# Building the S5 input matrices of six units on GpSimd instead of VectorE, in halves, with their transposes later on TensorE

## The chip, the cores and the metric

One core of a Trainium2 chip runs one program. Its engines are TensorE (PE in the profile: matrix products and transposes, with PEld for weight loads), VectorE (DVE), ScalarE (ACT), GpSimd (POOL) and SyncE (SP, which here only issues DMAs). Each engine takes its own instructions in order and waits on semaphores for the others. The metric is device time in microseconds for the whole program. Before the change: 1237.72 us, the median of three runs (1236.06 to 1237.88).

## The reference, cut to what matters

The program is a two-layer decoder trunk on 512 tokens of width 1024: an S5 state-space mixer, a gated FFN, stick-breaking attention and a second FFN. The change lies in the S5 mixer alone. It has 64 groups of 16 channels, each with 64 complex diagonal states:

```python
u = (h @ w_in).reshape(bsz, seq, N_GROUPS, SSM_GROUP)
mag = jnp.exp(a_re * dt)
ab_re, ab_im = mag * jnp.cos(a_im * dt), mag * jnp.sin(a_im * dt)
...
bb_re = f_re[..., None] * b_re - f_im[..., None] * b_im
bb_im = f_re[..., None] * b_im + f_im[..., None] * b_re
bu_re = jnp.einsum('blgh,gph->blgp', u, bb_re)
bu_im = jnp.einsum('blgh,gph->blgp', u, bb_im)
...
_, _, s_re, s_im = lax.associative_scan(combine, (a_seq_re, a_seq_im, bu_re, bu_im), axis=1)
y = (jnp.einsum('blgp,ghp->blgh', s_re, c_re) - jnp.einsum('blgp,ghp->blgh', s_im, c_im)
     + d_skip * u)
y = jax.nn.gelu(y.reshape(bsz, seq, D_SSM))
z = y @ w_glu
return z[..., :D_MODEL] * jax.nn.sigmoid(z[..., D_MODEL:])
```

## The kernel before

The scan is not run token by token. The 512 tokens are cut into 64 chunks of 8. Within a chunk everything is a matrix product with matrices made from the powers of the state factors: `b` with powers 1 to 8 gives the matrix that turns 8 inputs into a chunk's contribution to the state, `c` with powers 0 to 7 the one that turns a state into 8 outputs, and both together a small Toeplitz matrix for the part inside the chunk. Only the states from chunk to chunk are scanned.

The work is split into eight units n = 0 to 7 of eight groups each. For one unit:

- `op_b(n)` makes the input matrices. `products` multiplies `b3` (real, imaginary and a combination) by `pw3` (powers, 1 to 8) into a tile k of 1536 elements a partition; `sums` adds pairs of its thirds into bn, 1024 elements (a complex product with three real ones). Both on VectorE.
- `bt_(n, 0)` and `bt_(n, 1)` transpose the real and the imaginary half of bn on TensorE into PSUM bank kb; ScalarE copies each to a tile bts. `v_(n)` then multiplies bts with the inputs u8.
- `op_c(n)` makes cm in the same way from `c3`; `kk(n)` makes the Toeplitz kernel from cm (also in bank kb), ScalarE copies it into kx, `kx_(n)` adds the skip term on VectorE and sends it through DRAM (ks) into the matrix m by DMAs on SP.
- `states(n)` on VectorE: p (v turned by the table tb), wv, the scan rv with the decay tile mt, p again, then xv, the states at the chunk starts.
- `y_in(n)` (u8 with m) and `y_state(n)` (xv with cm) fill the output bank y on TensorE; ScalarE applies the gelu; `y_turn` transposes back, ScalarE splits the result into yh and yl, with a product yt<-yh,nid between them in `y_low`.

TensorE's own filler work is the product u = h @ w_in (`u` in the profile) and later the first part of the gated output product (`gl`). `fill(k)` puts k steps of it at a place; the table F says how many at four places of each unit, after the states (F[n][0]), after `y_state`, after `y_turn` and after `y_low`.

In the loop over n, the order on TensorE, VectorE and ScalarE is exactly the order in which the code is written (a manual schedule). GpSimd and SP are not in it: their order is set by the framework's scheduler. Unit n of the loop runs kk and v of unit n + 1, states and outputs of unit n, and op_b, bt_ and op_c of unit n + 2; before the change the five steps of `states(n)` and the two of `op_b(n + 2)` take turns. Units 0 and 1 are prepared ahead of the loop. bn has one buffer, so bn of a unit can be written only when the transposes of the unit before have read it. GpSimd, before the change, only writes zeros (the first part of kx, the first column of each block of mt and xv, once a unit) and issues the loads of w_in (wi) and w_glu (wvr).

Of the kernel before, what the change touches and what calls it, by code (L numbers as in the profile page):

```python
# [7 lines left out]
F32 = mybir.dt.float32  # L8
# [5 lines left out]
MUL, ADD, SUB, MAX, MIN = ALU.mult, ALU.add, ALU.subtract, ALU.max, ALU.min  # L14
# [3 lines left out]
P = 128  # L18
# [24 lines left out]
def bc(ap, axis, shape):  # L43
    return ap.unsqueeze(axis).to_broadcast(shape)
# [3 lines left out]
def trunk(ctx: ExitStack, tc: tile.TileContext, A, out):  # L48
    nc = tc.nc
    V, SC, PE, GP = nc.vector, nc.scalar, nc.tensor, nc.gpsimd  # L50
# [32 lines left out]
    def T(name, dt=F32, tag=None):  # L83
        if tag in TP:
            return tp.tile([P, S], dt, tag=tag, name=name, bufs=TP[tag])
        pool, bufs = cur["w"]
        return pool.tile([P, S], dt, tag=tag, name=name, bufs=bufs[tag])
# [4 lines left out]
    def wide(name, n, tag):  # L92
        pool, bufs = cur["w"]
        return pool.tile([P, n * S], F32, tag=tag, name=name, bufs=bufs[tag])
# [16 lines left out]
    def tt(o, a, b, op, eng=None):  # L111
        (eng or V).tensor_tensor(out=o, in0=a, in1=b, op=op)  # L112
# [128 lines left out]
    def s5(st_next):  # L241
        banks_by_tag(st=1, u=2, g=2, kb=1, v=1, y=1)
        with tc.tile_pool(name="s5", bufs=1) as sp, ExitStack() as wctx:
            def L(name, shape, bufs=None, dt=F32):
                return sp.tile([P] + shape, dt, name=name, **({"bufs": bufs} if bufs else {}))
# [6 lines left out]
            def halves(t):  # L252
                return t[:, 0:S], t[:, S:2 * S]
# [4 lines left out]
            b3, c3 = L("b3", [32, 3, 16]), L("c3", [32, 3, 16])  # L258

            def v4(t, a=4):  # L260
                return t.rearrange("p (a b) -> p a b", a=a)
# [90 lines left out]
            def fill(n):  # L352
                for _ in range(n):
                    next(pe)
# [43 lines left out]
            zc, k, r, p = s32(), s32(), s32(), s32()  # L398
# [73 lines left out]
            pw3 = L("pw3", [32, 3, 9])  # L472
# [39 lines left out]
            mg8 = L("mg8", [32])  # L512
# [13 lines left out]
            V.memset(tb[:, 1, :, 0:1], 0.0)  # L526
            sp2 = wctx.enter_context(tc.tile_pool(name="s5w", bufs=2))

            sh8 = [P, 4, 8, 16]

            def v5(t):
# [34 lines left out]
            def products(m3, pw3, n, e0):  # L566

                pr = slice(4 * n, 4 * n + 4)
                k3 = wide("k", 3, "k")
                sh = [P, 12, 8, 16]  # L570
                tt(k3.rearrange("p (a e h) -> p a e h", a=12, e=8), bc(m3[:, pr].rearrange("p a t h -> p (a t) h"), 2, sh),
                   bc(pw3[:, pr].rearrange("p a t e -> p (a t) e")[:, :, e0:e0 + 8], 3, sh), MUL)
                return k3.rearrange("p (a t c) -> p a t c", a=4, t=3)

            def sums(o, k3):

                o4 = o.rearrange("p (r a c) -> p r a c", r=2, a=4)
                tt(o4, bc(k3[:, :, 0], 1, [P, 2, 4, P]), k3[:, :, 1:3].rearrange("p a t c -> p t a c"), ADD)
# [8 lines left out]
            def kk(n):  # L587

                cmr, cmn = unit[n]["c"]
                bk = B("kk", "kb")  # L590
                for q in range(4):
                    o = bk[32 * q:32 * q + 32, 0:128]
                    mm(o, bdr[:, 4 * n + q], v4(cmr)[:, q], True, False)
                    mm(o, bdi[:, 4 * n + q], v4(cmn)[:, q], False, True)
                kx = sp2.tile([P, 240], F32, name="kx", bufs=1)
                GP.memset(kx[:, 0:112], 0.0)
                SC.copy(out=kx[:, 112:240], in_=bk[:, 0:128])
                unit[n]["kx"] = kx

# [14 lines left out]
            def op_b(n):  # L614

                unit[n] = {}
                k3 = products(b3, pw3, n, 1)
                yield
                bn = wide("bn", 2, "bn")
                sums(bn, k3)  # L620
                unit[n]["b"] = halves(bn)

            def bt_(n, i):
                pb = B("bt", "kb")
                for q in range(4):
                    PE.transpose(v4(pb)[:, q], v4(unit[n]["b"][i])[:, q], ident)
                bt = T("bts", tag="bt")
                SC.copy(out=bt, in_=pb)
                unit[n].setdefault("bt", []).append(bt)
# [10 lines left out]
                               v4(bts[ri])[:, q, 64 * g2:64 * g2 + 64], u83[:, 2 * q + g2], True, True)  # L640
                unit[n]["v"] = vb

            decay = {}

            def decays(n):

                decay[n] = sp2.tile([P, 256], F32, name="mt", bufs=1)
                m4 = v4(decay[n])
                SC.copy(out=m4, in_=bc(mg8[:, 4 * n:4 * n + 4], 2, [P, 4, 64]))
                GP.memset(m4[:, :, 0:1].rearrange("p q o -> p (q o)"), 0.0)  # L650

            def states(n):

                pr = slice(4 * n, 4 * n + 4)
                vb = unit[n].pop("v")
                turn = tb[:, :, pr].rearrange("p t q c -> p t (q c)")
                sh2 = [P, 2, 2, 256]
                p = wide("p", 2, "p")
                p4 = p.rearrange("p (t r c) -> p t r c", t=2, r=2)
                a1, a2 = p4[:, 0], p4[:, 1]  # L660
                tt(p4, bc(v4(vb, 2), 1, sh2), bc(turn, 2, sh2), MUL)
                yield
                wv = T("wv", tag="wv")
                tt(wv[:, 0:256], a1[:, 0], a2[:, 1], ADD)
                tt(wv[:, 256:512], a1[:, 1], a2[:, 0], SUB)
                yield
                rv = T("rv", tag="rv")
                for ri in range(2):
                    c = slice(256 * ri, 256 * ri + 256)
                    V.tensor_tensor_scan(out=rv[:, c], data0=decay[n], data1=wv[:, c], initial=0.0, op0=MUL, op1=ADD)  # L670
                if n + 1 < KT:
                    decays(n + 1)
                yield
                p = wide("p", 2, "p")
                p1, p2 = halves(p)
                tt(p.rearrange("p (t r c) -> p t r c", t=2, r=2), bc(v4(rv, 2), 1, sh2), bc(turn, 2, sh2), MUL)
                yield
                xv = T("xv", tag="xv")
                xv4 = xv.rearrange("p (r q c) -> p r q c", r=2, q=4)
                GP.memset(xv4[:, :, :, 0:1].rearrange("p r q o -> p (r q) o"), 0.0)  # L680
                r1 = p1.rearrange("p (r q c) -> p r q c", r=2, q=4)
                r2_ = p2.rearrange("p (r q c) -> p r q c", r=2, q=4)
                tt(xv4[:, 0, :, 1:64], r1[:, 0, :, 0:63], r2_[:, 1, :, 0:63], SUB)
                stt(xv4[:, 1, :, 1:64], r1[:, 1, :, 0:63], -1.0, r2_[:, 0, :, 0:63], MUL, SUB)

                unit[n]["x"] = xv4
# [36 lines left out]
            def y_low(yt, yh, yl):  # L723
                mm(yt, nid, yh, False, False)
                SC.copy(out=yl, in_=yt)
                ys.append((yh, yl))

            def run(gen, n=99):
                for _ in range(n):
                    if next(gen, True) is True:  # L730
                        return

            run(op_b(0))
            op_c(0)
            kk(0)
            evac()
# [5 lines left out]
            run(table, TAB0)  # L742
            evac()
            v_(0)
            run(op_b(1))
            fill(PRE[3])
            bt_(1, 0)
            bt_(1, 1)
# [5 lines left out]
            fill(PRE[4])  # L754
            evac()
            decays(0)
            with tc.manual_schedule(engines={E.PE, E.DVE, E.Activation}):
                for n in range(KT):
                    more = n + 2 < KT
                    if n + 1 < KT:  # L760
                        kk(n + 1)
                        v_(n + 1)
                    if n and n + 1 < KT:
                        turn_products(n + 1)
                    y_in(n)
                    st, cb = states(n), op_b(n + 2) if more else iter(())
                    for i in range(5):
                        run(st, 1)
                        run(cb, 1)
                        if i == 2:  # L770
                            if n + 1 < KT:
                                kx_(n + 1)
                            prep_lo()
                        if i == TSUM and n + 1 < KT:
                            turn_sums(n + 1)
                    fill(F[n][0])
                    y8 = y_state(n)
                    if more:
                        bt_(n + 2, 0)
                    evac(n == 0)  # L780
                    if more:
                        op_c(n + 2)
                    fill(F[n][1])
                    yy = y_turn(y8)
                    if more:
                        bt_(n + 2, 1)
                    fill(F[n][2])
                    y_low(*yy)
                    fill(F[n][3])
                    if n:  # L790
                        prep_hi(1)
# [699 lines left out]
```

## Time and profile before

| | before |
|---|---|
| median of three runs | 1237.72 us |
| profiled execution: device time | 1236.96 us |
| its span in the trace | 1235.2 us |
| granted TensorE clock | 0.997 |
| the loop over the units | about 58 to 155 us of the span |

In the profile, an instruction is named by line, engine, operation and its tiles, output and inputs (`bn<-k`). Line 112 is the helper `tt` (two-input VectorE instruction), 109 `stt`, 106 `mm`; so tiles tell more than lines. A busy time is the time in which an engine has an instruction under way; an entry in square brackets at the end of a row is the idle time before the instruction and what ended it. Starts of consecutive instructions overlap a little, so the cost of an instruction in a full queue is the distance from its start to the next start. In the tables by stretch, the columns are the stretch, its length, and for PE, PEld, DVE, ACT and POOL the busy time with the number of instructions, then the granted clock, the DMA share and GB/s.

### The profile page before, as it was taken

The numbers are of one execution on the slowest core, as the hardware profiler recorded it, in microseconds if no ns is written. First come the engines' busy times: TensorE is split into PE (matmuls) and PEld (weight loads), VectorE is DVE, ScalarE is ACT, GpSimd is POOL, SyncE is SP. The second block draws the span as 40 slices with busy tenths as digits, with TensorE's granted clock in tenths as the row PEclk, the third lists the DMA queues.
The fourth block names the chain that finished last, engine by engine and source line by source line (L and its number), as shares of the span: only waits on it lengthen the run. The fifth ranks groups of instructions, "written<-read, shape, count | busy, mean of one in ns | idle before, by whom it ended". The sixth has DMA issues, their size and how long they took to land.

```text
span 1235.2 us, 16227 instructions
## 1 busy us (share of the span) xinstructions
PE 1207.6 (98%) x6411; PEld 982.8 (80%) x6411; DVE 809.6 (66%) x1284; ACT 539.3 (44%) x866; POOL 24.2 (2%) x65
## 2 busy tenths in 40 slices
PE   7989999999999999999999999999999999999995
PEld 3457788788888888888889898888888888888884
DVE  7999764665435635557878989878655346536554
ACT  5234453433223323334577878765433233323331
POOL 1011020000000000000000000000000000000000
PEclk9999999999999999999999999999999999999998
DMA  5565443233233233233211211123233232332322
GB/s 199 150 166 140 122 124 98 86 102 98 90 102 99 82 106 101 92 91 100 76 51 53 82 55 48 39 86 103 86 102 97 91 103 86 91 113 88 94 75 69
DMA packets 55068, 118.47 MB, mean 96 GB/s; under 512 B 12912, under 2 KB 28528, under 8 KB 54992
## 3 DMA queue, kind: packets, MB, share of 16 engines
q1 hardware_dynamic: 50880, 105.55, 27.9%
q0 software_dynamic: 3248, 11.54, 3.1%
q8 instruction: 50, 0.82, 0.3%
q10 hardware_dynamic: 864, 0.35, 0.1%
q14 instruction: 26, 0.21, 0.1%
HBM read 109.03 MB, written 8.39 MB: 95 GB/s over the span
## 4 chain that ended last, share of the span: by engine, by line
PE 89%; DVE 8%; ACT 1%; issue 1%; DMA 1%; SPq 0%; DVEq 0%; ACTq 0%
PE fd L106 20%; PE fu L106 19%; PE fg L106 19%; PE kqb L106 7%; PE gl L106 6%; PE z L106 5%; PE ob L106 5%; PE v L106 4%; DVE k L112 2%; DVE p L112 1%; PE u L106 1%; PE y L106 1%; DVE cm L112 1%; DVE u L112 1%; DVE rv L670 1%
## 5 line engine op out<-in xcount | busy, mean ns | idle before, releaser
L106 PE MATMUL fd<-ah,wdh 128*128 128x512 f32 (+1 forms) x359 | 140.5, 391 | 0.0
L106 PE MATMUL fd<-ah,wdl 128*128 128x512 f32 (+1 forms) x359 | 139.2, 388 | 0.0
L106 PE MATMUL fd<-al,wdh 128*128 128x512 f32 (+1 forms) x359 | 137.9, 384 | 0.0
L112 DVE TENSOR_TENSOR x<-x,fd 128x512 f32<-128x512 f32 (+1 forms) x49 | 33.1, 676 | 119.8 <-PE fd L106 119.8
L157 ACT CAST wuh<-wur 128x1024 fp32r<-128x1024 f32 x44 | 46.4, 1054 | 134.4 <-PE fg L106 118.0
L157 ACT CAST wdh<-wdr 128x896 fp32r<-128x896 f32 (+1 forms) x48 | 47.1, 982 | 128.0 <-PE fd L106 98.2
L112 DVE TENSOR_TENSOR g<-fg,rb 128x512 f32<-128x512 f32 x44 | 30.4, 691 | 96.3 <-PE fg L106 93.5
L106 PE MATMUL fu<-xh,wuh 128*128 128x512 f32 x220 | 86.0, 391 | 0.0
L106 PE MATMUL fg<-xh,wgl 128*128 128x512 f32 x220 | 85.8, 390 | 0.0
L106 PE MATMUL fg<-xh,wgh 128*128 128x512 f32 x220 | 85.7, 390 | 0.0
L106 PE MATMUL fg<-xl,wgh 128*128 128x512 f32 x220 | 85.6, 389 | 0.0
L106 PE MATMUL fu<-xh,wul 128*128 128x512 f32 x220 | 85.6, 389 | 0.0
L106 PE MATMUL fu<-xl,wuh 128*128 128x512 f32 x220 | 85.6, 389 | 0.0
L112 DVE TENSOR_TENSOR u<-fu,rb 128x512 f32<-128x512 f32 x44 | 30.4, 691 | 80.5 <-PE fu L106 80.5
L106 PE MATMUL fu<-xhl,wuh 128*128 128x512 f32 x264 | 81.8, 391 | 0.0
L106 PE MATMUL fg<-xhl,wgh 128*128 128x512 f32 x264 | 81.5, 389 | 0.0
L106 PEld LDWEIGHTS fd<-ah,wdl 128*128 128x128 f32 x359 | 67.4, 188 | 15.2
L106 PEld LDWEIGHTS fd<-al,wdh 128*128 128x128 f32 x359 | 67.4, 188 | 14.8 <-issue 0.2
L106 PEld LDWEIGHTS fd<-ah,wdh 128*128 128x128 f32 x359 | 67.5, 188 | 13.2 <-issue 0.2
L157 ACT CAST wgh<-wgr 128x1024 fp32r<-128x1024 f32 x44 | 46.3, 1053 | 71.0 <-PE fd L106 33.0
L106 PE MATMUL u<-xg,wi 128*128 128x512 f32 x128 | 63.5, 628 | 7.5 <-ACT xg L270 7.5
L109 DVE SCALAR_TENSOR_TENSOR acc<-g,cw,acc 128x511 f32<-128x511 f32 x88 | 65.8, 747 | 2.4 <-ACT acc L832 0.9
(247 smaller groups left out, 2799.1 us busy)
## 6 DMA issues: line engine op xcount, KB each, us to landing
wgr<-in_w_up SPq DMA_DIRECT2D x44, 512.0 KB, 3.5
wur<-in_w_up SPq DMA_DIRECT2D x44, 512.0 KB, 3.5
wdr<-in_w_dn SPq DMA_DIRECT2D x32, 448.0 KB, 3.3
wdr<-in_w_dn SPq DMA_DIRECT2D x16, 512.0 KB, 3.5
wvr<-in_w_glu POOLq DMA_DIRECT2D x12, 512.0 KB, 3.8
ks<-kx SPq DMA_DIRECT2D x32, 128.0 KB, 2.5
m<-ks SPq DMA_DIRECT2D x8, 512.0 KB, 4.1
awr<-in_w_k SPq DMA_DIRECT2D x8, 512.0 KB, 3.5
```

The lines of the kernel that those rows point to most:

```text
L106: PE.matmul(o, lhsT=lhsT, rhs=rhs, start=start, stop=stop, skip_group_check=True)
L109: (eng or V).scalar_tensor_tensor(out=o, in0=a, scalar=s, in1=b, op0=op0, op1=op1)
L112: (eng or V).tensor_tensor(out=o, in0=a, in1=b, op=op)
L157: SC.copy(out=hi, in_=raw)
L670: V.tensor_tensor_scan(out=rv[:, c], data0=decay[n], data1=wv[:, c], initial=0.0, op0=MUL, op1=ADD)
```

## The change

For n = 2 to 7, `op_b` makes bn on GpSimd in two halves (two of the unit's four state blocks each): a product kp of 768 elements into a buffer of its own, and a sum of 512 elements into half of bn. For n = 0 and 1 VectorE still does it. kx, mt and xv become tiles that exist once: their zeros are written once ahead of the loop, and the per-unit zero fills on GpSimd are gone; the ScalarE copy into mt leaves the zero column out (63 of 64 columns). In the loop, `op_b(n + 2)` stands ahead of `states(n)`; `bt_(n + 2, 0)` moves from behind `y_state` to behind `y_turn`, and `bt_(n + 2, 1)` from there to behind `y_low`. F is unchanged.

```diff
@@ -526,6 +526,10 @@
             V.memset(tb[:, 1, :, 0:1], 0.0)
             sp2 = wctx.enter_context(tc.tile_pool(name="s5w", bufs=2))
 
+            zeroed = {"kx": sp2.tile([P, 240], F32, name="kx", bufs=1), "mt": sp2.tile([P, 256], F32, name="mt", bufs=1)}
+            GP.memset(zeroed["kx"][:, 0:112], 0.0)
+            GP.memset(v4(zeroed["mt"])[:, :, 0:1].rearrange("p q o -> p (q o)"), 0.0)
+
             sh8 = [P, 4, 8, 16]
 
             def v5(t):
@@ -592,8 +596,7 @@
                     o = bk[32 * q:32 * q + 32, 0:128]
                     mm(o, bdr[:, 4 * n + q], v4(cmr)[:, q], True, False)
                     mm(o, bdi[:, 4 * n + q], v4(cmn)[:, q], False, True)
-                kx = sp2.tile([P, 240], F32, name="kx", bufs=1)
-                GP.memset(kx[:, 0:112], 0.0)
+                kx = zeroed["kx"]
                 SC.copy(out=kx[:, 112:240], in_=bk[:, 0:128])
                 unit[n]["kx"] = kx
 
@@ -614,11 +617,20 @@
             def op_b(n):
 
                 unit[n] = {}
-                k3 = products(b3, pw3, n, 1)
-                yield
                 bn = wide("bn", 2, "bn")
-                sums(bn, k3)
                 unit[n]["b"] = halves(bn)
+                if n < 2:
+                    sums(bn, products(b3, pw3, n, 1))
+                    return
+                for i in range(2):
+                    pr = slice(4 * n + 2 * i, 4 * n + 2 * i + 2)
+                    kp = sp2.tile([P, 768], F32, name="kp", bufs=1)
+                    tt(kp.rearrange("p (a e h) -> p a e h", a=6, e=8),
+                       bc(b3[:, pr].rearrange("p a t h -> p (a t) h"), 2, [P, 6, 8, 16]),
+                       bc(pw3[:, pr].rearrange("p a t e -> p (a t) e")[:, :, 1:9], 3, [P, 6, 8, 16]), MUL, GP)
+                    k3 = kp.rearrange("p (a t c) -> p a t c", a=2, t=3)
+                    o4 = bn.rearrange("p (r a c) -> p r a c", r=2, a=4)[:, :, 2 * i:2 * i + 2]
+                    tt(o4, bc(k3[:, :, 0], 1, [P, 2, 2, P]), k3[:, :, 1:3].rearrange("p a t c -> p t a c"), ADD, GP)
 
             def bt_(n, i):
                 pb = B("bt", "kb")
@@ -640,14 +652,10 @@
                                v4(bts[ri])[:, q, 64 * g2:64 * g2 + 64], u83[:, 2 * q + g2], True, True)
                 unit[n]["v"] = vb
 
-            decay = {}
-
             def decays(n):
 
-                decay[n] = sp2.tile([P, 256], F32, name="mt", bufs=1)
-                m4 = v4(decay[n])
-                SC.copy(out=m4, in_=bc(mg8[:, 4 * n:4 * n + 4], 2, [P, 4, 64]))
-                GP.memset(m4[:, :, 0:1].rearrange("p q o -> p (q o)"), 0.0)
+                m4 = v4(zeroed["mt"])
+                SC.copy(out=m4[:, :, 1:64], in_=bc(mg8[:, 4 * n:4 * n + 4], 2, [P, 4, 63]))
 
             def states(n):
 
@@ -667,7 +675,7 @@
                 rv = T("rv", tag="rv")
                 for ri in range(2):
                     c = slice(256 * ri, 256 * ri + 256)
-                    V.tensor_tensor_scan(out=rv[:, c], data0=decay[n], data1=wv[:, c], initial=0.0, op0=MUL, op1=ADD)
+                    V.tensor_tensor_scan(out=rv[:, c], data0=zeroed["mt"], data1=wv[:, c], initial=0.0, op0=MUL, op1=ADD)
                 if n + 1 < KT:
                     decays(n + 1)
                 yield
@@ -675,9 +683,7 @@
                 p1, p2 = halves(p)
                 tt(p.rearrange("p (t r c) -> p t r c", t=2, r=2), bc(v4(rv, 2), 1, sh2), bc(turn, 2, sh2), MUL)
                 yield
-                xv = T("xv", tag="xv")
-                xv4 = xv.rearrange("p (r q c) -> p r q c", r=2, q=4)
-                GP.memset(xv4[:, :, :, 0:1].rearrange("p r q o -> p (r q) o"), 0.0)
+                xv4 = zeroed["xv"].rearrange("p (r q c) -> p r q c", r=2, q=4)
                 r1 = p1.rearrange("p (r q c) -> p r q c", r=2, q=4)
                 r2_ = p2.rearrange("p (r q c) -> p r q c", r=2, q=4)
                 tt(xv4[:, 0, :, 1:64], r1[:, 0, :, 0:63], r2_[:, 1, :, 0:63], SUB)
@@ -730,7 +736,7 @@
                     if next(gen, True) is True:
                         return
 
-            run(op_b(0))
+            op_b(0)
             op_c(0)
             kk(0)
             evac()
@@ -742,7 +748,7 @@
             run(table, TAB0)
             evac()
             v_(0)
-            run(op_b(1))
+            op_b(1)
             fill(PRE[3])
             bt_(1, 0)
             bt_(1, 1)
@@ -754,6 +760,8 @@
             fill(PRE[4])
             evac()
             decays(0)
+            zeroed["xv"] = T("xv", tag="xv")
+            GP.memset(zeroed["xv"].rearrange("p (r q c) -> p r q c", r=2, q=4)[:, :, :, 0:1].rearrange("p r q o -> p (r q) o"), 0.0)
             with tc.manual_schedule(engines={E.PE, E.DVE, E.Activation}):
                 for n in range(KT):
                     more = n + 2 < KT
@@ -763,10 +771,11 @@
                     if n and n + 1 < KT:
                         turn_products(n + 1)
                     y_in(n)
-                    st, cb = states(n), op_b(n + 2) if more else iter(())
+                    if more:
+                        op_b(n + 2)
+                    st = states(n)
                     for i in range(5):
                         run(st, 1)
-                        run(cb, 1)
                         if i == 2:
                             if n + 1 < KT:
                                 kx_(n + 1)
@@ -775,17 +784,17 @@
                             turn_sums(n + 1)
                     fill(F[n][0])
                     y8 = y_state(n)
-                    if more:
-                        bt_(n + 2, 0)
                     evac(n == 0)
                     if more:
                         op_c(n + 2)
                     fill(F[n][1])
                     yy = y_turn(y8)
                     if more:
-                        bt_(n + 2, 1)
+                        bt_(n + 2, 0)
                     fill(F[n][2])
                     y_low(*yy)
+                    if more:
+                        bt_(n + 2, 1)
                     fill(F[n][3])
                     if n:
                         prep_hi(1)
```

On VectorE, unit 1 of the loop, from the cm of the preparation to the second p (k and bn are the input matrices of unit 3, pw the powers):

```order
 L112 TENSOR_TENSOR cm<-k 128x1024
 L112 TENSOR_TENSOR p<-v,tb 128x1024
-L112 TENSOR_TENSOR k<-b_91,pw_255 128x1536
 L112 TENSOR_TENSOR wv<-p 128x256 x2
-L112 TENSOR_TENSOR bn<-k 128x1024
-L670 SCALAR_TENSOR_TENSOR rv<-mt,wv 128x256 x2
+L678 SCALAR_TENSOR_TENSOR rv<-mt,wv 128x256 x2
 L109 SCALAR_TENSOR_TENSOR kx<-par,kx 128x16
 L112 TENSOR_TENSOR p<-rv,tb 128x1024
```

k and bn are gone from between the steps of the states; the scan rv only has another line number. The same holds in units 0 and 2 to 5.

On TensorE, the end of unit 0, from `y_state` (y<-cm,xv) to kk of the next unit:

```order
 L106 MATMUL y<-cm,xv 64x128 x16
-L626 MATMUL bt<-ident,bn 128x128 x4
-L106 MATMUL yt<-ident,y_674 64x64 x16
-L626 MATMUL bt<-ident,bn 128x128 x4
+L106 MATMUL yt<-ident,y_673 64x64 x16
+L638 MATMUL bt<-ident,bn 128x128 x4
 L106 MATMUL u<-xg,wi 128x512 x3
 L106 MATMUL yt<-yh,nid 128x512
+L638 MATMUL bt<-ident,bn 128x128 x4
 L106 MATMUL kk<-cm,bdr 32x128
```

The first four transposes moved behind yt, the second four behind yt<-yh,nid, so that in this unit they stand directly ahead of kk.

On GpSimd after the change, from the second wi load of the loop's preparation to the first half of unit 3 (numbers kept: kp_621 and kp_624 are the halves of unit 2, kp_770 the first half of unit 3):

```order
L292 DMA wi_443<-in_w_in 128x1024
L112 ISA
L112 TENSOR_TENSOR kp_621<-b3_91,pw3_255 128x768
L292 DMA wi_523<-in_w_in 128x1024
L292 DMA wi_651<-in_w_in 128x1024
L292 DMA wi_850<-in_w_in 128x1024
L112 TENSOR_TENSOR bn_620<-kp_621 128x2x256
L112 TENSOR_TENSOR kp_624<-b3_91,pw3_255 128x768
L112 TENSOR_TENSOR bn_620<-kp_624 128x2x256
L112 TENSOR_TENSOR kp_770<-b3_91,pw3_255 128x768
L340 DMA wvr_852<-in_w_glu 128x2x256 x2
L112 TENSOR_TENSOR bn_769<-kp_770 128x2x256
```

Where zero fills stood between the loads there are now four arithmetic instructions a unit, with the loads between them in the queue; ISA is a library row that comes once, ahead of the first of them.

## The prediction

> **What bounds the kernel now.** I read the table of busy time by unit first, then the waits of TensorE, then the instructions in order of time. n below counts the units of the S5 stage from 0, as the code does, so the change's "units 3 to 8" are n = 2 to 7. In the first fence the columns are the stretch, its length, and the busy time of PE, PEld, DVE, ACT and POOL; each stretch but the last runs from the first VectorE instruction of one unit to that of the next, and the last covers n = 6 and 7.
>
> ```profile
> PE 1207.6 (98%) x6411; PEld 982.8 (80%) x6411; DVE 809.6 (66%) x1284; ACT 539.3 (44%) x866; POOL 24.2 (2%) x65
> 58.40:72.55 14.15, 12.36 (x151) 8.04 (x150) 14.08 (x19) 4.92 (x14) 1.59 (x4) 1.00 0.71 196
> 72.55:83.72 11.17, 10.03 (x113) 6.08 (x113) 11.10 (x17) 4.93 (x15) 0.41 (x3) 1.00 0.52 137
> 83.72:96.02 12.30, 11.48 (x149) 7.56 (x151) 12.23 (x17) 6.34 (x16) 3.46 (x8) 1.00 0.63 180
> 96.02:109.31 13.29, 12.32 (x182) 9.02 (x183) 13.22 (x18) 6.28 (x17) 1.44 (x5) 1.00 0.46 114
> 109.31:122.90 13.59, 13.06 (x160) 10.43 (x161) 13.56 (x20) 6.72 (x17) 1.50 (x5) 1.00 0.51 136
> 122.90:134.00 11.10, 9.42 (x137) 7.37 (x133) 11.03 (x17) 5.51 (x15) 0.41 (x3) 1.00 0.44 122
> 134.00:155.00 21.00, 20.92 (x283) 16.72 (x278) 11.50 (x22) 7.88 (x20) 1.28 (x4) 1.00 0.44 127
> ```
>
> Over the whole kernel TensorE is 98% busy, but in units 0 to 5 VectorE has no idle time at all (14.08 of 14.15 us, 11.10 of 11.17, and so on), while TensorE lacks 1.79, 1.14, 0.82, 0.97, 0.53 and 1.68 us: 6.9 us in the six units. After 134 us TensorE is full again. So VectorE sets the pace of six units, by a narrow margin. The waits of TensorE between 58.4 and 155 us say the same:
>
> ```profile
> PE y L106 <- DVE xv L112: 6.1, 6, 1.7
> PE y L106 <- DMA m<-ks: 0.7, 1, 0.7
> ```
>
> TensorE waits once in each of six units, for xv. Nothing this stage can gain exceeds the 6.9 us; what it can lose has no such limit, because each microsecond by which xv of unit 5 comes later goes to the end whole. Here is unit 1 on VectorE (start, duration, instruction, output and inputs):
>
> ```profile
> 72.55 1.22 DVE L112 TENSOR_TENSOR p<-v,tb 128x1024 f32<-128x1024 f32 x1
> 73.68 1.75 DVE L112 TENSOR_TENSOR k<-b,pw 128x1536 f32<-128x1536 f32 x1
> 75.35 0.75 DVE L112 TENSOR_TENSOR wv<-p 128x256 f32<-128x256 f32 x2
> 76.02 1.21 DVE L112 TENSOR_TENSOR bn<-k 128x1024 f32<-128x1024 f32 x1
> 77.16 1.26 DVE L670 TENSOR_TENSOR_SCAN rv<-mt,wv 128x256 f32<-128x256 f32 x2
> 78.34 0.20 DVE L109 SCALAR_TENSOR_TENSOR kx<-par,kx 128x16 f32<-128x16 f32 x1
> 78.47 1.21 DVE L112 TENSOR_TENSOR p<-rv,tb 128x1024 f32<-128x1024 f32 x1
> 79.72 0.42 DVE L112 TENSOR_TENSOR xv<-p 128x252 f32<-128x252 f32 x1
> 80.06 0.41 DVE L109 SCALAR_TENSOR_TENSOR xv<-p 128x252 f32<-128x252 f32 x1
> 80.39 0.48 DVE L112 TENSOR_TENSOR tb<-tq 128x128 f32<-128x128 f32 x2
> 80.79 1.75 DVE L112 TENSOR_TENSOR k<-c,pwc 128x1536 f32<-128x1536 f32 x1
> 82.57 1.23 DVE L112 TENSOR_TENSOR cm<-k 128x1024 f32<-128x1024 f32 x1
> 83.72 1.22 DVE L112 TENSOR_TENSOR p<-v,tb 128x1024 f32<-128x1024 f32 x1
> ```
>
> The work of one unit ahead, k from b and pw and then bn, stands between p and xv of the present unit.
>
> **The change part by part.** *What VectorE loses.* From start to start, k costs 75.35 - 73.68 = 1.67 us and bn 77.16 - 76.02 = 1.14 us: 2.81 us a unit, six times, 16.9 us.
>
> *What GpSimd gets.* Two products of 768 elements a partition (kp) and two sums of 512 (bn) a unit. No row shows GpSimd doing arithmetic, or reading SBUF at all: it fills with constants and issues DMAs. The nearest row is a fill of 1024 elements:
>
> ```profile
> L496 POOL MEMSET bdr<- 128x1024 f32 x1 | 1.0, 970 | 0.0
> ```
>
> That is 0.95 ns for one written element. The cheap end for an instruction with two inputs is this rate, its three streams side by side: 0.73 us for kp, 0.49 for bn, 2.4 us a unit. The dear end is the three streams one after another, 2.84 ns an element: 2.18 and 1.45 us, 7.3 a unit. I take two reads in sequence with the write beside them, 1.9 ns: 1.46 and 0.97 us, 4.86 a unit, since the fill row bounds one stream and an engine that has drawn no input here gives no reason to count on two at once. A page gives a price too: the Trainium skill, "GPSIMD Engine Reference", section 3, "Performance versus the Vector engine", lists 4497 ns for a two-input add of 2048 fp32 elements, by which I estimate 1.69 and 1.12 us, 5.6 us a unit.
>
> *Does that time lie beside VectorE?* This decides the sign, and no row shows it. One end: the two engines run side by side and GpSimd's 4.86 us are hidden in a unit of 11 us or more. Other end: while one reads SBUF the other cannot, and every microsecond of GpSimd is one that VectorE stands still. In the rows above p<-v,tb, with one input in PSUM, and p<-rv,tb, with both in SBUF, take 1.22 and 1.21 us for 1024 elements: VectorE draws two full streams from SBUF, in all its instructions of this unit but p<-v,tb. If GpSimd's stream has to come out of the same capacity, there is hardly a moment in a unit when it is free. I take the second end as likelier. The Trainium skill, "SBUF — State Buffer", section "Who interferes with whom", states just that: a VectorE instruction with two SBUF inputs and a GpSimd instruction that reads SBUF exclude each other for a whole instruction; no run so far shows it.
>
> *The sum.* VectorE stands still for GpSimd's time and sheds its own: 6 x 4.86 - 16.9 = +12.3 us at xv of unit 5, with nothing left in which TensorE could hide it. (The first of the kp lies ahead of the loop, where VectorE is on the chain too, so it counts.) Some of it can fall beside the two instructions that read PSUM, p<-v,tb (1.13 us start to start, each unit) and the one in this row, in units 0, 3 and 4:
>
> ```profile
> L112 DVE TENSOR_TENSOR u<-u,rb 128x512 f32<-128x512 f32 x8 | 8.6, 1072 | 0.0
> ```
>
> A unit's GpSimd work is released by the transposes that end a TensorE unit, when VectorE has usually passed these, so I count one of each, -2.1. By the page's price the sum before this would be 6 x 5.6 - 16.9 = +16.7 us, an estimate.
>
> *The transposes (bt) later on TensorE.* Unit 0, TensorE and ScalarE:
>
> ```profile
> 68.13 1.96 PE L106 MATMUL y<-cm,xv 64*64 64x128 f32 x32 [1.69 <-DVE xv L112]
> 70.02 0.66 PE L626 MATMUL bt<-ident,bn 128*128 128x128 f32 x4
> 70.13 0.60 ACT L708 ACTIVATE y<-y 128x512 f32<-128x512 f32 x1 [3.37 <-PE y L106]
> 70.78 1.15 PE L106 MATMUL yt<-ident,y 64*64 64x64 f32 x32
> 71.86 0.66 PE L626 MATMUL bt<-ident,bn 128*128 128x128 f32 x4
> 72.35 2.74 PE L106 MATMUL u<-xg,wi 128*128 128x512 f32 x6
> 72.93 0.58 ACT L628 COPY bts<-bt 128x512 f32<-128x512 f32 x1 [0.37 <-ACT yh L720]
> 74.53 0.79 PE L106 MATMUL yt<-yh,nid 128*128 128x512 f32 x1
> 75.25 0.45 PE L106 MATMUL kk<-cm,bdr 128*32 128x128 f32 x8
> 75.36 0.58 ACT L725 CAST yl<-yt 128x512 fp32r<-128x512 f32 x1 [1.84 <-PE yt L106]
> ```
>
> The first bt filled the wait for the gelu (0.60 us); in unit 0 nothing replaces it, 0.5 us. The second bt now stands after yt<-yh,nid, directly ahead of the next unit's kk, which uses the same PSUM bank and so waits for the bts copy; that copy stands behind yl on ScalarE. yl and bts take 0.58 each, some 1.3 us with the hand-overs, against 0.5 of bt: 0.8 us where no filler stands between, that is after units 0, 2 and 5. While VectorE sets the pace, the first two vanish in TensorE's wait for xv; only the one after unit 5 counts, +0.9 with its extra 0.1 of hand-over.
>
> *The rest.* POOL's DMA issues now queue behind arithmetic. Their cover:
>
> ```profile
> 35.66 0.53 POOL L292 DMA_DIRECT2D wi<-in_w_in  x1 [6.33 <-PE u L106]
> 52.20 1.12 PE L106 MATMUL u<-xg,wi 128*128 128x512 f32 x2
> 64.16 0.72 POOL L340 DMA_DIRECT2D wvr<-in_w_glu  x1 [11.96 <-PE u L106]
> 86.97 1.05 ACT L157 CAST wvh<-wvr 128x1024 fp32r<-128x1024 f32 x1
> wvr<-in_w_glu POOLq DMA_DIRECT2D x12, 512.0 KB, 3.8
> ```
>
> The wi load that the first kp precedes is used 16.5 us after its issue, the first wvr load 22.8 us after; the last row, of the page's DMA issues, has 3.8 us to landing, so each has over 12 us to spare, enough for the library row (ISA) ahead of the first kp as well. The dropped fills of kx, mt and xv cost VectorE no visible wait before; zero. SP's kx and m transfers follow kx, which sits behind the same chain as xv and shifts with it.
>
> Together 12.3 - 2.1 + 0.9 = **+11.1 us**. The profiled execution took 1236.96 us (span 1235.2), 0.76 under the median of 1237.72; on the median the forecast is **1249 us**.
>
> **The rivals.** *A, side by side: faster.* VectorE's unit 1 falls to 11.17 - 2.81 = 8.4 us, below TensorE's 10.03, so TensorE sets the pace and its 6.9 us of idle go. Against that stand 0.5 and 3 x 0.8 us from the transposes, and some 0.5 us where kx on ScalarE waits behind a wvh cast: -3.5 us, 1234.2; at best 1231. For it: no row shows the two engines disturbing one another. Against it: GpSimd here has only written.
>
> *B, no change.* The engines exclude one another, but GpSimd runs near its cheap end or mostly beside p<-v,tb and u. The turning point is 6 x (GpSimd per unit) = 16.9, 2.8 us a unit, close to the 2.4 of the cheap end: 1237.7 within 2.5 us. Against it: two inputs at the rate of one written stream.
>
> *C, GpSimd itself late: slower without any exclusion.* From about 10.3 us a unit (4 ns an element, above my dear end) bn would come after TensorE wants it; at 5 ns, 12.8 us a unit, five units by 2.5 us: +12, 1250.
>
> That the work does not leave VectorE can be excluded: the order shows k and bn gone from its units.
>
> **How the numbers follow.** Exclusion with a loss 0.56, A 0.30, B 0.09, C 0.05. The forecast's own range is 1241 to 1257; its dear end, 6 x 7.3 - 16.9 = +26.9, lies near 1264, and I leave most of that out; its lower end is a price near 1.4 ns an element. With A's best the range is **1231 to 1257**. About 0.2% (2.5 us) is what a measurement of this kernel tells from no change. Faster: most of A, 0.27; same: the weak part of A and most of B, 0.13; slower: 0.60.
>
> **What would show it.** Right: VectorE's instructions in units 1 to 5 that read twice from SBUF start late or run long while a GpSimd kp or bn is in progress, p<-v,tb does not, units grow to some 13 to 16 us, and TensorE's waits for xv grow from 6.1 to over 15 us. Kp and bn near 1.5 and 1 us would show the price right. Wrong: units of 10 us, VectorE idle at kx for TensorE's kk, and waits for xv near zero (A); or TensorE waiting for bn (C).

## The result and the profile after

The changed kernel takes 1249.6 us (median of four runs, 1249.08 to 1249.75) against 1237.29 us before in the same comparison: ratio 1.0100, 95% interval 1.0083 to 1.0118. It is slower by 12.3 us, where 11.1 had been forecast. The profiled execution has a span of 1248.0 us, 12.8 more than before. Busy times of the whole span:

```profile
PE 1210.8 (97%) x6411; PEld 984.3 (79%) x6411; DVE 815.3 (65%) x1272; ACT 538.8 (43%) x866; POOL 61.7 (5%) x68
```

GpSimd is busy for 37.5 us longer, the time in which it is itself held included. VectorE, which was to lose 16.9 us of work, is busy for 5.7 us longer than before with twelve instructions fewer. The units, cut as in the prediction at the first VectorE instruction of each (stretch, length, busy PE, PEld, DVE, ACT, POOL, granted clock, DMA share, GB/s):

```profile
60.23:74.47 14.24, 12.50 (x147) 7.83 (x146) 14.17 (x16) 4.80 (x14) 7.07 (x6) 1.00 0.61 173
74.47:87.44 12.97, 10.21 (x109) 6.14 (x107) 12.80 (x15) 4.15 (x13) 6.81 (x4) 0.89 0.67 181
87.44:102.76 15.32, 12.58 (x166) 8.20 (x167) 12.76 (x15) 6.19 (x16) 10.22 (x8) 0.98 0.45 132
102.76:118.19 15.43, 12.45 (x174) 9.11 (x171) 13.94 (x16) 6.69 (x17) 8.59 (x6) 1.00 0.35 81
118.19:133.75 15.56, 13.02 (x128) 10.52 (x127) 15.42 (x18) 6.28 (x17) 7.28 (x6) 0.89 0.44 112
133.75:146.41 12.66, 11.25 (x175) 8.59 (x176) 10.38 (x14) 5.34 (x15) 4.99 (x3) 1.00 0.43 118
```

Units 1 to 5 take 1.6 to 3.0 us more than before, unit 0 the same, and the loop starts 1.83 us later (60.23 against 58.40). Two things are new: VectorE has idle time in units 2, 3 and 5, and TensorE's granted clock drops in units 1 and 4. The waits in the loop that grew or are new, of TensorE and of VectorE (before the change TensorE's six waits for xv were 6.1 us, and the other two did not exist):

```profile
PE y L106 <- DVE xv L112: 11.4, 6, 2.7
PE kk L106 <- ACT bts L640: 2.2, 3, 0.7
DVE kx L109 <- ACT kx L600: 5.8, 3, 2.4
```

Where VectorE's time went is best seen in unit 1, with VectorE and GpSimd in one order of time:

```profile
76.40 2.30 DVE L678 TENSOR_TENSOR_SCAN rv<-mt,wv 128x256 f32<-128x256 f32 x2
78.62 1.40 DVE L109 SCALAR_TENSOR_TENSOR kx<-par,kx 128x16 f32<-128x16 f32 x1
79.95 1.21 DVE L112 TENSOR_TENSOR p<-rv,tb 128x1024 f32<-128x1024 f32 x1
81.26 1.29 DVE L112 TENSOR_TENSOR xv<-p 128x252 f32<-128x252 f32 x1
82.48 1.71 DVE L109 SCALAR_TENSOR_TENSOR xv<-p 128x252 f32<-128x252 f32 x1
84.11 0.48 DVE L112 TENSOR_TENSOR tb<-tq 128x128 f32<-128x128 f32 x2
...
76.86 1.28 POOL L112 TENSOR_TENSOR bn<-kp 128x512 f32<-128x512 f32 x1 [9.33 <-PE bt L638]
78.23 1.76 POOL L112 TENSOR_TENSOR kp<-b,pw 128x768 f32<-128x768 f32 x1
80.07 2.21 POOL L112 TENSOR_TENSOR bn<-kp 128x512 f32<-128x512 f32 x1
82.36 1.55 POOL L112 TENSOR_TENSOR kp<-b,pw 128x768 f32<-128x768 f32 x1
```

kx, 16 columns and 0.20 us before, takes 1.40: it ends at 80.02, when kp of GpSimd ends (79.99). Then p runs at its usual 1.21, and this time bn is the one that waits: 2.21 us instead of 1.28. xv waits for that bn (82.28), and the second xv (1.71 instead of 0.41) for the next kp. The two engines take turns, one instruction each. Unit 0 shows the other case. There GpSimd's burst begins beside p<-v,tb and u<-u,rb, each with one input in PSUM, and all four take their usual time:

```profile
60.23 1.23 DVE L112 TENSOR_TENSOR p<-v,tb 128x1024 f32<-128x1024 f32 x1
61.37 1.09 DVE L112 TENSOR_TENSOR u<-u,rb 128x512 f32<-128x512 f32 x1
...
60.18 1.27 POOL L112 TENSOR_TENSOR bn<-kp 128x512 f32<-128x512 f32 x1 [6.66 <-DVE tb L112]
61.53 1.50 POOL L112 TENSOR_TENSOR kp<-b,pw 128x768 f32<-128x768 f32 x1
```

Over the loop, the six groups that changed and one that did not; before first (58.40 to 134), then after (60.23 to 146.41); the figures behind the bar are busy time and mean duration:

```profile
L670 DVE TENSOR_TENSOR_SCAN rv<-mt,wv 128x256 f32<-128x256 f32 x12 | 7.6, 671 | 0.0
L112 DVE TENSOR_TENSOR p<-rv,tb 128x1024 f32<-128x1024 f32 x6 | 7.3, 1215 | 0.0
L112 DVE TENSOR_TENSOR wv<-p 128x256 f32<-128x256 f32 x12 | 4.5, 417 | 0.0
L112 DVE TENSOR_TENSOR xv<-p 128x252 f32<-128x252 f32 x6 | 2.5, 421 | 0.2
L109 DVE SCALAR_TENSOR_TENSOR xv<-p 128x252 f32<-128x252 f32 x6 | 2.5, 414 | 0.0
L109 DVE SCALAR_TENSOR_TENSOR kx<-par,kx 128x16 f32<-128x16 f32 x6 | 1.2, 206 | 0.0
L112 DVE TENSOR_TENSOR p<-v,tb 128x1024 f32<-128x1024 f32 x7 | 8.5, 1218 | 0.1
```

```profile
L678 DVE TENSOR_TENSOR_SCAN rv<-mt,wv 128x256 f32<-128x256 f32 x12 | 12.3, 1062 | 0.0
L112 DVE TENSOR_TENSOR p<-rv,tb 128x1024 f32<-128x1024 f32 x6 | 9.4, 1572 | 0.0
L112 DVE TENSOR_TENSOR wv<-p 128x256 f32<-128x256 f32 x12 | 7.3, 646 | 0.2
L109 DVE SCALAR_TENSOR_TENSOR kx<-par,kx 128x16 f32<-128x16 f32 x6 | 6.8, 1136 | 5.8 <-ACT kx L600 5.8
L112 DVE TENSOR_TENSOR xv<-p 128x252 f32<-128x252 f32 x6 | 6.5, 1079 | 0.6
L109 DVE SCALAR_TENSOR_TENSOR xv<-p 128x252 f32<-128x252 f32 x6 | 3.8, 626 | 0.0
L112 DVE TENSOR_TENSOR p<-v,tb 128x1024 f32<-128x1024 f32 x6 | 7.3, 1219 | 0.1
```

The six stretched groups grew from 25.6 to 46.1 us: 20.5 us. p<-v,tb kept its 1.22 us; of its six, the one of unit 0 is the one that stood beside GpSimd's arithmetic. So the account of VectorE in the loop is -16.9 (work shed) + 20.5 (stretch) + 5.8 (kx waits for ScalarE) = +9.4, of the +10.6 by which the six units grew; 1.2 us stay without a name. The 10.6 and the 1.8 us ahead of the loop make 12.4 of the 12.8 us by which the span grew.

### The profile page after: what moved, and what is told of

Same layout as the page of the kernel before. It is cut to its first block, busy times and chain, and to the rows that moved or that the text cites. A ratio compares the mean times of both kernels' runs of the same rounds, so it can differ in the third digit from the quotient of the medians.

```text
span 1248.0 us, 16185 instructions
## 1 busy us (share of the span) xinstructions
PE 1210.8 (97%) x6411; PEld 984.3 (79%) x6411; DVE 815.3 (65%) x1272; ACT 538.8 (43%) x866; POOL 61.7 (5%) x68
## 4 chain that ended last, share of the span: by engine, by line
PE 89%; DVE 8%; ACT 1%; issue 1%; DMA 1%; SPq 0%; DVEq 0%; ACTq 0%
PE fd L106 19%; PE fu L106 19%; PE fg L106 19%; PE kqb L106 7%; PE gl L106 7%; PE z L106 5%; PE ob L106 5%; PE v L106 4%; DVE p L112 1%; PE y L106 1%; DVE k L112 1%; PE u L106 1%; DMA x<-in_xT 1%; DVE u L112 1%; PE yt L106 1%
```

## The experiments

All are variants of the changed kernel, each timed against the kernel before; that kernel's median in the three sets was 1237.55, 1237.21 and 1237.44 us. The theory is exclusion: while GpSimd reads SBUF, VectorE instructions with two SBUF inputs stand still. The rivals are the late transposes, GpSimd coming late in itself, and, from the new rows, TensorE's clock.

### Transposes early again, arithmetic still on GpSimd

```diff
                     y8 = y_state(n)
+                    if more:
+                        bt_(n + 2, 0)
                     evac(n == 0)
...
                     yy = y_turn(y8)
                     if more:
-                        bt_(n + 2, 0)
+                        bt_(n + 2, 1)
                     fill(F[n][2])
                     y_low(*yy)
-                    if more:
-                        bt_(n + 2, 1)
```

> The changed kernel with one part undone: the transposes stand where they stood before the change; the GpSimd arithmetic and the kept zeros stay. Theory 'exclusion' (GpSimd's 33 us of arithmetic, 12 x (1.50 + 1.28), stop VectorE instructions that read twice from SBUF): the loss stays, 1247 to 1251 us, and the waits of VectorE's kx for ScalarE (6.5 us in the changed kernel) shrink while the stretched VectorE instructions grow. Rival 'late transposes' (the loss comes from bts, kk and kx being later in each unit): 1237 to 1242 us.

Measured: 1246.06 us, ratio 1.0066 (1.0050 to 1.0083). Most of the loss stays, but 3.5 us go: between what the two theories said. VectorE's busy time is the same as in the changed kernel (814.8 against 815.3 us), so the stretch did not grow; TensorE's kk no longer waits for bts (2.2 us there), and VectorE waits less for kx:

```profile
DVE kx L109 <- ACT kx L600: 4.3, 2, 2.5
```

That is over a stretch reaching to 175 us, in which the changed kernel has 6.5 us; in the six units alone it is 4.3 against 5.8. So the late transposes are a part of the loss, the smaller one. The run ranges of the two kernels (1245.99 to 1246.55, 1249.08 to 1249.75) do not meet, but in the two traces only 2.3 us of the difference lie in the six units (83.91 against 86.18 us).

### Arithmetic back on VectorE, transposes late

```diff
-                if n < 2:
-                    sums(bn, products(b3, pw3, n, 1))
-                    return
-                for i in range(2):
...
+                k3 = products(b3, pw3, n, 1)
+                yield
+                bn = wide("bn", 2, "bn")
+                sums(bn, k3)
...
+                    st, cb = states(n), op_b(n + 2) if more else iter(())
                     for i in range(5):
                         run(st, 1)
+                        run(cb, 1)
```

> The changed kernel with the arithmetic back on VectorE, as whole units between the steps of the states; late transposes and kept zeros stay. Exclusion: 1237 to 1240 us (about 1 us for the kk after unit 5 that waits for a bts copy). Late transposes: 1243 us or more. Kept zeros as a cause would show here too.

Measured: 1237.82 us, ratio 0.9999 (0.9990 to 1.0008). The late transposes alone cost nothing that can be measured.

### Kept zeros alone

The arithmetic on VectorE as above and the transposes early as above; what is left of the change is that kx, mt and xv keep their zeros.

> The kernel before with the kept zeros alone (arithmetic on VectorE, transposes at their old places). It completes the square of GpSimd or VectorE by late or early transposes. Exclusion: 1236.5 to 1238 us, no change. If the zero fills on GpSimd had cost something before: under 1236 us.

Measured: 1237.22 us, ratio 1.0000 (0.9991 to 1.0010). With this the square is full: VectorE with early and late transposes 1237.2 and 1237.8, GpSimd 1246.1 and 1249.6. GpSimd costs about 9 us by itself, and late transposes cost 3.5 us, but only beside it. By which way they cost it there is not shown.

### Fills in the place of arithmetic

```diff
-                    tt(kp.rearrange(...), bc(b3...), bc(pw3...), MUL, GP)
...
-                    tt(o4, bc(k3[:, :, 0], 1, [P, 2, 2, P]), k3[:, :, 1:3].rearrange(...), ADD, GP)
+                    for _ in range(5):
+                        GP.memset(o4, 0.0)
```

> The changed kernel with every GpSimd product and sum replaced by fills: five fills of 512 elements into each half of bn, 10 x 0.49 = 4.9 us a unit, released by the same transposes; kp is not computed, so bn of units 2 to 7 holds zeros and the output is not the reference's. GpSimd is as busy as before on the same buffers but reads nothing. Exclusion by reading: no VectorE instruction is stretched, VectorE sheds its 2.8 us a unit, and the time falls to 1232 to 1237 us. Rival 'GpSimd late' (bn comes too late for the transposes, whatever it reads): 1247 us or more. Rival 'any GpSimd access to SBUF stops VectorE': 1245 us or more, with stretched VectorE instructions.

Measured: 1232.35 us, ratio 0.9956 (0.9941 to 0.9971). GpSimd is nearly as long occupied (a unit's fills take 4.72 us, the arithmetic undisturbed 5.56), on the same bn and behind the same transposes, but reads nothing: 17.3 us less than the changed kernel, 5 us less than the kernel before. TensorE's wait for xv is gone; in the loop it has left only kk (2.2 us) and, in another row, 0.7 us, and it is VectorE that waits:

```profile
PE kk L106 <- ACT bts L636: 2.2, 3, 0.7
DVE kx L109 <- ACT kx L600: 10.9, 6, 2.8
```

This excludes that GpSimd's writes stop VectorE, and speaks against work that came late, of which the changed kernel's own rows show nothing either: no wait of TensorE in its loop is for bn. The time lies between the side-by-side rival's best (1231) and its middle (1234.2).

### Every GpSimd instruction twice

```diff
+                    for _ in range(2):
                         tt(kp.rearrange(...), ..., MUL, GP)
...
+                    for _ in range(2):
                         tt(o4, ..., ADD, GP)
```

> The changed kernel with every GpSimd product and sum issued twice, same result. GpSimd's undisturbed time grows by 33 us. Exclusion: nearly all of it reaches the end, 1272 to 1284 us. If GpSimd's time were hidden and the loss came from elsewhere: 1249 to 1253 us. If GpSimd only costs where it comes late for the transposes: between, 1253 to 1262 us.

Measured: 1276.79 us, ratio 1.0316 (1.0298 to 1.0333). 27.2 us more for another 33 us of GpSimd. TensorE waits 24.6 us for xv, and its mean clock over most of the loop falls to 0.86:

```profile
60.00:170.00 110.00, 81.62 (x875) 56.88 (x874) 106.54 (x88) 33.91 (x92) 82.77 (x56) 0.86 0.39 104
```

How much of the 27 us is clock I did not separate. GpSimd's second 33 us go to the end nearly whole, but not one to one; of the first, 17.3 us did, measured against the fills.

### One half on GpSimd, one on VectorE

```diff
+                for i, eng in enumerate((GP, V)):
...
-                       ..., MUL, GP)
+                       ..., MUL, eng)
+                    if i == 1:
+                        yield
...
-                    tt(o4, ..., ADD, GP)
+                    tt(o4, ..., ADD, eng)
```

> The changed kernel with only the first half of each unit's product and sum on GpSimd; VectorE makes the second half between the steps of the states, as the whole was made before. GpSimd gets 2.8 us a unit, VectorE sheds 1.4. Exclusion, in proportion: 1241 to 1245 us. If half of the work fits beside the instructions that read PSUM (1.1 to 2.1 us a unit): 1236 to 1239 us.

Measured: 1242.21 us, ratio 1.0039 (1.0024 to 1.0054). 5.0 us for half of the work against 12.3 for all. So half of the work costs a little less than half of the loss. TensorE waits 7.1 us for xv and its busy time is 1207.3 us, as before the change, so here the clock did not drop.

### One-input copies on GpSimd

```diff
-                    tt(kp.rearrange(...), ..., MUL, GP)
+                    for _ in range(2):
+                        GP.tensor_copy(out=kp, in_=b3[:, 0:16].rearrange("p a t h -> p (a t h)"))
...
-                    tt(o4, ..., ADD, GP)
+                    for _ in range(2):
+                        GP.tensor_copy(out=o4, in_=kp[:, 0:512].rearrange(...))
```

> The changed kernel with every GpSimd product and sum replaced by two copies with one SBUF input (kp from the raw b3, halves of bn from kp; the input matrices of units 2 to 7 are not computed, so the output is not the reference's). At the rate of a fill that is 4 x 0.73 + 4 x 0.49 = 4.9 us a unit, as in the kernel with fills. If any GpSimd read of SBUF excludes a two-input VectorE instruction: 1243 to 1250 us, with VectorE instructions stretched as in the changed kernel. If only two-input GpSimd instructions do: 1231 to 1235 us, as with fills.

Measured: 1241.16 us, ratio 1.0030 (1.0019 to 1.0042): between the two forecasts, 8.8 us above the fills. The stretch is there, one copy at a time. Here k from c, 1.75 us before, stands beside two copies:

```profile
80.89 2.37 DVE L112 TENSOR_TENSOR k<-c,pwc 128x1536 f32<-128x1536 f32 x1
...
80.69 3.26 POOL L629 COPY kp<-b 128x768 f32<-128x768 f32 x2
```

Two copies take 3.26 us here and 1.79 where less stands in their way. So a GpSimd instruction with a single SBUF input excludes as well. Why more of its time than of the products' stays free (17.3 us of VectorE busy time over the fills, against 21.1) I did not separate.

### Fillers moved ahead of y_state

```diff
-F = ((4, 0, 3, 0), (1, 1, 1, 1), (2, 1, 1, 0), (3, 1, 1, 3), (3, 2, 1, 1), ...
+F = ((4, 0, 3, 0), (2, 1, 1, 0), (2, 1, 1, 0), (4, 1, 1, 2), (5, 1, 1, 0), ...
```

> The changed kernel with fillers moved ahead of y_state: F[1] from (1,1,1,1) to (2,1,1,0), F[3] from (3,1,1,3) to (4,1,1,2), F[4] from (3,2,1,1) to (5,1,1,0); the same TensorE work, less of it between xv of a unit and kk of the next. The changed kernel's trace shows two waits for xv of 2.0 and 2.5 us after which TensorE's granted clock is 0.50 for 3.2 and 3.6 us. If those waits and the long way from xv to kk to kx make up what is over the pure exclusion: 1244 to 1248 us, fewer stretches at 0.50, and kx waits under 5 us. If the clock and kx play no part: 1249 to 1250 us.

Measured: 1249.0 us, ratio 1.0096 (1.0080 to 1.0113): no gain that its runs (1247.72 to 1252.22) could tell from the changed kernel, though the kx waits fell as in the first forecast. VectorE's waits for kx fell to 3.8 us, but its busy time rose to 817.1 us (815.3 in the changed kernel), and kk now waits 3.7 us for bts instead of 2.2.

The waits for kx are no sum of their own: while VectorE waits there, GpSimd works undisturbed, and what VectorE does not wait it is stretched. TensorE's busy time (1210.5 us, against 1210.8) shows that the clock was no better either.

### TensorE kept busy

```diff
+IDLE = (0, 5, 9, 8, 9, 4)
...
                     fill(F[n][0])
+                    if 0 < n < 6:
+                        idle = B("idle", "kb")
+                        for _ in range(IDLE[n]):
+                            mm(idle, nid, ys[n - 1][0], True, True)
                     y8 = y_state(n)
```

> The changed kernel with products of no use (5, 9, 8, 9, 4 of them in units 1 to 5, some 0.23 us each) put on TensorE ahead of y_state, in the time in which it waits for xv; their output, in bank kb, is read by nobody. If TensorE's clock of 0.50 after its long waits costs time at the end: the granted clock stays at 1.00 through the loop, TensorE's busy time without these products falls by about 3 us against the changed kernel, and the time to 1246 to 1248 us. If the slow stretches lie beside VectorE's work anyway: 1249 to 1250 us with a full clock. If the products come in the way of y_state: above 1250 us.

Measured: 1247.84 us (1247.62 to 1248.40), ratio 1.0084 (1.0069 to 1.0098). The clock is at 1.00 in every stretch of the loop; the useless products are 35 for 9.7 us, and without them TensorE is busy for 1207.5 us, as before the change.

```profile
PE 1217.2 (98%) x6446; PEld 989.3 (79%) x6446; DVE 817.5 (66%) x1272; ACT 538.9 (43%) x866; POOL 62.8 (5%) x68
```

Against the changed kernel's 1249.6 that is 1.8 us less, with run ranges that do not meet, although the two intervals against the kernel before overlap. In the two traces the six units take 84.02 instead of 86.18 us, 2.2 us less. So the slow clock costs the change about 2 us at the end, of 3.2 us of TensorE time.

No version beat both kernels in a way that could be used. The fills show that 5 us are there for whoever relieves VectorE of this work without reading SBUF from GpSimd; no run here tries another engine for it. That TensorE could form the sums by accumulating its transposes was not tried either.

## Why the prediction was right, and where it was not

**The bound** was read rightly: VectorE by a narrow margin in units 0 to 5, no gain beyond some 7 us (the fills got 5), losses without a limit.

**The deciding step**, whether GpSimd's time lies beside VectorE's, was chosen rightly, and is shown: by the turns in unit 1, by p<-v,tb and u<-u,rb unchanged beside GpSimd in unit 0, by the fills, by the doubling. The Trainium skill's rule in "SBUF — State Buffer", section "Who interferes with whom", holds in each particular of it that was tried: two SBUF inputs stand still, one SBUF and one PSUM input do not, GpSimd writes do no harm, one-input reads do.

**GpSimd's price** was too low. Undisturbed, bn while VectorE waited for kx and kp ahead of the kx that it then held, the two take:

```profile
91.33 1.28 POOL L112 TENSOR_TENSOR bn<-kp 128x512 f32<-128x512 f32 x1 [1.68 <-PE bt L638]
92.69 1.50 POOL L112 TENSOR_TENSOR kp<-b,pw 128x768 f32<-128x768 f32 x1
```

That is 5.56 us a unit, 33.4 in all, not 4.86 and 29.2: 4.2 us too little. The estimate from the Trainium skill, "GPSIMD Engine Reference", section 3, "Performance versus the Vector engine", 5.6, was the better one in sum, though not for each (1.69 and 1.12).

**The overlap**, -2.1, was far too small. VectorE was stretched by 20.5 us in the loop, and by some 1.3 ahead of it, out of 33.4: 11.6 us of GpSimd's time did no direct harm. The one p<-v,tb and one u<-u,rb that were counted are there, some 2.1 us in unit 0. Not counted were some 4.4 us in which GpSimd works while VectorE waits for kx; the other 5 us I did not separate.

**VectorE without waits** is the step that failed. The sum took each microsecond that VectorE sheds as one gained, and let the first two late transposes "vanish in TensorE's wait for xv". But kx stands ahead of xv in VectorE's order, and it comes from kk over ScalarE. Before, k and bn filled the time up to it, and kx started 5.79 us after the first instruction of units 2, 3 and 5 without a wait. Now VectorE is there earlier and waits in these three units, 5.8 us in all:

```profile
93.02 1.19 DVE L109 SCALAR_TENSOR_TENSOR kx<-par,kx 128x16 f32<-128x16 f32 x1 [2.39 <-ACT kx L600]
107.28 1.36 DVE L109 SCALAR_TENSOR_TENSOR kx<-par,kx 128x16 f32<-128x16 f32 x1 [1.32 <-ACT kx L600]
139.05 1.25 DVE L109 SCALAR_TENSOR_TENSOR kx<-par,kx 128x16 f32<-128x16 f32 x1 [2.10 <-ACT kx L600]
```

These starts are 5.58, 4.52 and 5.30 us after those of their units: kx is no later in its unit than before, VectorE is earlier. The fills show the same without any stretch: 10.9 us of waits for kx, and of the 16.9 us shed only 5 reach the end.

The late transposes are not the main cause of these waits; most of them come behind a unit with a slow clock. Here those of units 2 and 5 follow units 1 and 4 (0.89 and 0.89). With the transposes early, two waits are left, 4.3 us, in units 2 and 4, behind units 1 and 3 at 0.86 and 0.89; with the fillers moved, the one of 3.16 us, in unit 4, stands behind a unit at 0.88. With the transposes late but TensorE kept busy, the waits of units 2 and 5 are gone, and that of unit 3 stands as it was (the same source lines have numbers one higher there):

```profile
91.75 1.40 DVE L110 SCALAR_TENSOR_TENSOR kx<-par,kx 128x16 f32<-128x16 f32 x1
106.22 1.36 DVE L110 SCALAR_TENSOR_TENSOR kx<-par,kx 128x16 f32<-128x16 f32 x1 [1.32 <-ACT kx L601]
136.85 1.40 DVE L110 SCALAR_TENSOR_TENSOR kx<-par,kx 128x16 f32<-128x16 f32 x1
```

Units 2 and 5 take 14.12 and 11.67 us there, 1.2 and 1.0 less, not the 2.39 and 2.10 of the waits, since VectorE is stretched instead. The kk that waits for a bts copy does so where it was forecast, after units 0, 2 and 5, by 0.73 us each. Of the first two, the one in unit 1 vanished, and the one in unit 3 came with a wait for kx. So the 0.9 us for the transposes was too low as well (3.5 us in the medians, 2.3 in the six units of the traces); the way by which they cost that is open.

**The clock** was not in the sum at all: 3.2 us of TensorE time, about 2 us at the end, by way of the kx waits of units 2 and 5.

So the sum of 11.1 for a measured 12.3 is better than its terms: a price 4.2 us too low and an overlap 9.5 us too small, against 5.8 us of waits left out, a part of them the clock's. The range and the side were earned by the mechanism, the closeness was luck.

**The signs** came with two exceptions. TensorE's waits for xv grew from 6.1 to 11.9 us (11.4 and, for the second xv, 0.5), not to over 15; TensorE's other losses are 2.2 us for bts, 0.7 for the gelu and 3.2 by its clock. And "VectorE idle at kx", named as a sign of side by side, came together with the exclusion.

**The rivals.** A (side by side) is excluded in the changed kernel; its time is near what the fills took, 1232.35. B needed GpSimd at 2.8 us a unit; it has 5.56. C, lateness, is excluded by TensorE's waits, none of which is for bn. The loads on GpSimd's queue did no harm, as reckoned: no wait of TensorE in the loop names them.

## What to carry to other kernels

Work taken off a full VectorE and given to GpSimd is not beside it if both read SBUF: each GpSimd instruction takes its turn, so 2.81 us of VectorE work became 5.56 us of turns. Before such a move, look which VectorE instructions of the stage have one operand in PSUM, since only beside these, and in VectorE's waits, is GpSimd free. And ask what the engine that sets the pace will wait for once it has less to do: here it was kx, by way of TensorE and ScalarE, and part of the work shed went into that wait.

## What the runs showed of the hardware that I had not expected

TensorE's granted clock falls after quite short waits. In the changed kernel's unit 4, where it waits 2.54 us for xv (stretches of one microsecond; the figure ahead of the last two is the granted clock):

```profile
128.00:129.00 1.00, 0.00 (x0) 0.00 (x0) 0.90 (x3) 0.00 (x0) 0.44 (x1) 1.00 0.96 219
129.00:130.00 1.00, 0.97 (x10) 0.97 (x12) 1.00 (x4) 0.00 (x0) 0.00 (x0) 0.50 1.03 235
130.00:131.00 1.00, 1.00 (x12) 1.00 (x10) 1.00 (x2) 0.00 (x0) 0.00 (x0) 0.50 0.08 29
131.00:132.00 1.00, 1.00 (x13) 1.00 (x12) 1.00 (x1) 0.00 (x0) 0.00 (x0) 0.50 0.36 79
```

y_state there takes 3.60 us instead of 1.96. The same came in unit 1 after waits of 1.50 and 0.54 us, but not in units 2 and 3 after 2.74 and 2.25; what tells them apart is open. With the gaps filled, in the last experiment, the clock stayed at 1.00. The Trainium skill, "TensorE: Matmul & The Clock Gate", section "Why this matters for your kernels", puts the limit for idle gaps at about 3 us; here 2.54 was enough once, and two shorter waits in a row another time.

And a VectorE instruction with one small input was held too. Ahead of the loop, beside the first kp, sy with four columns takes 1.48 us instead of 0.16 and ends with kp. It takes 1.47 or 1.48 in all six kernels here that have this product beside it, and 0.16 in the other five. This is 1.3 of the 1.8 us by which the loop starts later; the other 0.5 is there before, at sv (28.06 instead of 27.56), ahead of all GpSimd arithmetic:

```profile
30.12 1.48 DVE L118 TENSOR_SCALAR sy<-sf 128x4 int32<-128x4 f32 x1
...
29.92 1.66 POOL L112 TENSOR_TENSOR kp<-b,pw 128x768 f32<-128x768 f32 x1
```
